# A two-layer hybrid attention block in float32: memory queries by way of DRAM, a scaling moved to ScalarE, two powers moved up, and the last tile cut 384 and 128

## The chip, the cores and the metric

The kernel runs on one core of a Trainium2 chip. The metric is the device time of one execution in microseconds (us). The profile is one execution taken by the hardware profiler. The engines are called PE (TensorE, with its weight loads as PEld), DVE (VectorE), ACT (ScalarE), POOL (GpSimd) and SP (SyncE, which here only issues transfers).

## What is computed

Two layers of a decoder trunk over 256 tokens of width 1024, everything in float32:

```python
h = rms_norm(x, norm_g[l])
q_a, k_a, v_a, q_h, f_h, i_h, q_m, z = jnp.split(h @ w_in[l], split_points, axis=-1)
# 8 heads x 64: QK-norm, partial rotary, causal softmax attention (one block of 256 keys)
qa = partial_rope(rms_norm(q_a, moba_q_norm[l]), positions)      # ka alike
o_a = moba_attention(qa, ka, va)
# 4 heads x 128: gated linear recurrence in chunks, then a norm of each head
o_h = rms_norm(hgrn2_chunkwise(q_h, f_h, i_h, lb_all[l]), hgrn_o_norm[l])
# 4 heads x 128: attention on 256 memory tokens
k_m, v_m = jnp.split(rms_norm(mem, mem_norm_g[l]) @ w_mem_kv[l], 2, axis=-1)
qm = rms_norm(q_m, mem_q_norm[l])                                # km alike
o_m = memory_attention(qm, km, v_m)                              # softmax(qm km^T / sqrt(128)) v_m
x = x + (jnp.concatenate([o_a, o_h, o_m], axis=-1) * jax.nn.silu(z)) @ w_out[l]
```

## The kernel before

**Weights.** All weights stream through the core once, in 60 chunks a layer of 128 x 1024 float32 (512 KB). Each takes the same road: SP loads it into `wr` (4 buffers; L177), ACT casts it to the rounded high part `wh` (3 buffers; L213, or L217 where a gain is folded in), DVE subtracts to get the low part `wl` (3 buffers; L227 or L231), and PE multiplies with both, so that high x high, low x high and high x low together give float32 accuracy. A chunk of `w_in` for a projection that is kept token by token (`group_b`, L292 to L294) takes 12 matmuls of 512 columns. The two gate projections at the end, ZA and ZM (`group_a`, L275), take 8 matmuls of 512 columns with `wh` and 8 of 256 with `wl` a chunk. The chunks of a layer, in order: 0 to 7 the memory's keys and values; 8 to 39 the projections F, Q, K, I, Q, Z of HGRN, the memory's queries (QM: 32 to 35) and VA (36 to 39); 40 to 43 ZA; 44 to 47 ZM; 48 to 59 `w_out` (L1443).

**What sets the order.** Each engine runs its instructions in the order in which they are written into its program. Generators for the side work (norms, rotary, recurrence, attention) are stepped between the matmul groups, and tables of the form `in_turn(a, b, c)` pin the order on DVE, ACT and POOL around named instructions: `("wl", c + 41)` is the low part of chunk 41 of layer `c / 60`, `("scale", 1, i)` a scaling of the second P, and so on.

**The memory's queries.** `g_qm` copies the QM projection to `qm` (L1246), takes sums of squares, and lets POOL raise the mean square to the power -1/2 (`rsq`, L702; `hgr` is the same for the recurrence's out-norm). `qm` holds a token per partition; the scores need a head's dimension per partition. So PE transposes it in 8 pieces of 128 x 128 (L1260, four for each half of the tokens) into a `sd` tile of PSUM, ACT casts the tile to `qmh` and DVE subtracts to `qml`. The 24 scores matmuls of a layer (L275, `sd<-kml,qmh` and the like) are written to run just after VA and within ZA.

**Trips through DRAM.** `across` (L85) turns other tensors: DVE transposes blocks of 32 x 32 within `src` into `blk` (L95), one transfer writes `blk` to a DRAM buffer `there` (L106), and four transfers of a quarter each bring it back in the turned layout (L111). All of a trip's transfers go by one queue, SP's or POOL's. The keys `kT` go by SP, and the queries `qT`, the recurrence's output `zh` and the softmax numerators P go by POOL. P comes in two halves of 128 x 1536 each (units 0 and 1); each is scaled by 1/sum (`ria`) on DVE in 8 pieces (L1178) ahead of its trip, and comes back as `PT`.

**Powers of K.** The key norm needs two powers on POOL (`rka`, L1081), one for each half of the tokens. In layer 0 POOL first finishes the rotary tables (L664 to L669), then raises both powers.

**The end.** In the last layer the last accumulator of `w_out` is cut into two parts of 256 columns, so that the first part's add (L1497) and output transfer start while PE works on the second (L1504).

Of the kernel before, what the change touches and what calls it, by code (L numbers as in the profile page):

```python
# [45 lines left out]
def hymba_kernel(ctx: ExitStack, tc: tile.TileContext, x, mem, mem_t, positions, w_in, w_out, w_mem_kv,  # L46
                 gains, moba_g, out):
    nc = tc.nc
# [39 lines left out]
    def across(dst, src, n, stage=None, free=None, name=None, q=None, behind=None, pace=(2, 4)):  # L88
# [21 lines left out]
        for c in (0, 2, 1, 3):  # L110
            ins = q.dma_start(dst[c * 32:c * 32 + 32], there[:, :, c].rearrange("q j r -> j q r"))  # L111
            if c == 2:
                yield
# [460 lines left out]
    def g_setup():  # L574
# [81 lines left out]
        for l in range(DEPTH):  # L656
            for q in (1, 0):
# [16 lines left out]
                if l == 0:  # L674
                    yield
# [201 lines left out]
    def g_hgrn(l):  # L877
# [60 lines left out]
        for m in (2, 8):  # L938
# [43 lines left out]
            nc.vector.tensor_tensor(Kn[:, :, 0:3], K4[:, :, 0:3], by(1, 3), op=OP.mult)  # L982
# [61 lines left out]
        for t in range(2):  # L1044
# [9 lines left out]
            yield  # L1054
        r = rsq("hg", ss, 8, 128)
# [12 lines left out]
    def g_qk(l, q, acc):  # L1068
# [8 lines left out]
        def spread(t):  # L1077
            t8 = slice(t * 8, t * 8 + 8)
            sumsq(ss[:, t8], acc[t], 8, "qk", t)
            nc.vector.tensor_scalar(ms[:, t8], ss[:, t8], 1.0 / 64, EPS, op0=OP.mult, op1=OP.add)  # L1080
            N["pow", t] = nc.gpsimd.tensor_tensor(r[:, t8], ms[:, t8], pw[:, :8], op=OP.pow)  # L1081
# [30 lines left out]
        else:  # L1112
            yield
            for t in range(2):
                k3 = heads(kr[:, t], 8)
                nc.vector.tensor_tensor(k3, k3, r[:, t * 8:t * 8 + 8][:, :, None].to_broadcast([128, 8, 64]),
                                        op=OP.mult)
# [41 lines left out]
    def g_moba_unit(l, u, P, mx):  # L1159
# [15 lines left out]
        for t in range(2):  # L1175
            for i in range(4):
                c = t * 4 + i
                N["scale", u, c] = nc.vector.tensor_scalar(P[:, i, kc[t]], P[:, i, kc[t]], ri[:, c:c + 1], None, op0=OP.mult)  # L1178
# [63 lines left out]
    def g_qm(l, acc):  # L1242
# [9 lines left out]
        yield 2  # L1252
        qmh = sb.tile([128, 4, 256], F32R, name="qmh", tag="ih", bufs=1)
        qml = sb.tile([128, 4, 256], F32R, name="qml", tag="hF", bufs=1)
        for t in range(2):
            ts = slice(t * 128, (t + 1) * 128)
            yield from room("sd")
            pt = side_tile()
            for h in range(4):
                N["qm turn", t, h] = nc.tensor.transpose(pt[:, h * 128:(h + 1) * 128], qm[:, t, h * 128:(h + 1) * 128],  # L1260
                                                         ident)
            N["qmh", t] = nc.scalar.copy(qmh[:, :, ts], heads(pt, 4))
            N["qml", t] = nc.vector.tensor_tensor(qml[:, :, ts], heads(pt, 4), qmh[:, :, ts].bitcast(F32), op=OP.subtract)
            rel()
        yield 2
# [95 lines left out]
    def order_of_attention(l):  # L1361
# [4 lines left out]
        in_turn(w("wl", 23), ("third", 8))  # L1366
# [3 lines left out]
        in_turn(w("wl", 26), ("decay", 8))  # L1370
# [11 lines left out]
        in_turn(w("wl", 37), w("wl", 38), ("across", f"turned0{l}"))  # L1382
        for h in range(4):
            in_turn(("mm", c + 37, 1, 1), ("qm turn", 1, h))
        if not l:
# [199 lines left out]
```

## Time and profile before

| | |
|---|---|
| median of 3 runs | 384.18 us (384.08 to 384.66) |
| the profiled execution | 384.07 us |
| its span in the profile | 382.3 us |
| PE busy | 377.0 us, 99% of the span |
| DVE, ACT, POOL busy | 322.7 us (84%), 251.0 us (66%), 113.5 us (30%) |
| moved by DMA | 87.64 MB, mean 229 GB/s |
| granted TensorE clock | 9 (of 9) in each of the 40 slices |

The profile's span runs from the first to the last recorded event; 1.8 us of the profiled execution's time lie outside it. Rows of the timeline, the chain of work that ended last and the groups of instructions give a start in us, a duration, the engine, the source line, and output<-inputs by the program's names. A group's row ends with the idle time in front of the group and who ended it.

### The profile page before, as it was taken

The page shows a single profiled execution, that of the slowest core. Times are in us where ns is not written, and L with a number is a line of the kernel's source. Part 1 is how long each engine was busy: PE and PEld are TensorE (multiplying, and loading weights), DVE is VectorE, ACT ScalarE, POOL GpSimd, SP SyncE. Part 2 cuts the span into 40 slices and gives each one's busy share as a digit, 9 for nine tenths or more (in the row PEclk, how much of TensorE's full clock was granted, in tenths as well). Part 3 has the DMA queues.
Part 4 walks back from the last instruction along what each step waited for, and adds up shares of the span by engine and source line. Part 5 has one row for each costly group of instructions (what it writes and reads, how often), then busy time and mean ns, then how long its engine had stood idle before and what let it go on. Part 6 is the DMA issues. An engine that isn't in the chain of part 4 may idle for free.

```text
span 382.3 us, 6807 instructions
## 1 busy us (share of the span) xinstructions
PE 377.0 (99%) x2431; PEld 317.6 (83%) x2431; DVE 322.7 (84%) x596; ACT 251.0 (66%) x428; POOL 113.5 (30%) x199
## 2 busy tenths in 40 slices
PE   8999999999999999999999999999999999999996
PEld 6888888878888888888888888888887888888885
DVE  4789979899879999967596989899897799998763
ACT  4988866449859839755366857455665993794540
POOL 3176889700700722320021030020043052225000
PEclk9999999999999999999999999999999999999999
DMA  8985795277923889996549668646766168999612
GB/s 268 418 319 180 229 308 167 111 256 227 294 106 120 269 275 330 333 256 227 172 171 286 213 210 245 238 135 227 261 220 223 55 247 262 321 303 318 204 53 110
DMA packets 27250, 87.64 MB, mean 229 GB/s; under 512 B 3792, under 2 KB 6224, under 8 KB 27216
## 3 DMA queue, kind: packets, MB, share of 16 engines
q1 hardware_dynamic: 22304, 71.31, 55.1%
q0 software_dynamic: 4624, 15.73, 13.9%
q8 instruction: 19, 0.31, 0.3%
q10 hardware_dynamic: 288, 0.15, 0.1%
q14 instruction: 15, 0.12, 0.1%
HBM read 76.18 MB, written 11.01 MB: 228 GB/s over the span
## 4 chain that ended last, share of the span: by engine, by line
PE 85%; POOL 9%; DVE 3%; issue 1%; DMA 1%; ACT 0%; DVEq 0%
PE acc L275 19%; PE acc L1443 17%; PE acc L312 12%; PE acc L292 9%; PE acc L293 9%; PE acc L294 9%; PE sd L275 5%; PE sd L279 4%; POOL rt L605 1%; POOL rt L606 1%; DMA gT<-in_gains_dram 1%; POOL mk L672 1%; POOL rtB L669 1%; POOL rk L721 1%; POOL rtA L666 1%
## 5 line engine op out<-in xcount | busy, mean ns | idle before, releaser
L213 ACT CAST wh<-wr 128x1024 fp32r<-128x1024 f32 x96 | 100.9, 1052 | 51.1 <-PE acc L275 15.6
L227 DVE TENSOR_TENSOR wl<-wr,wh 128x1024 fp32r<-128x1024 f32 x96 | 116.5, 1217 | 15.7 <-ACT wh L213 15.6
L293 PE MATMUL acc<-wl,hT 128*128 128x512 f32 x192 | 75.6, 394 | 0.0
L294 PE MATMUL acc<-wh,hT 128*128 128x512 f32 x192 | 74.8, 390 | 0.0
L292 PE MATMUL acc<-wh,hT 128*128 128x512 f32 x192 | 70.7, 396 | 0.0
L275 PE MATMUL acc<-hT,wh 128*128 128x512 f32 x256 | 63.9, 391 | 0.0
L275 PEld LDWEIGHTS acc<-hT,wh 128*128 128x128 f32 x256 | 46.4, 189 | 8.3
L292 PEld LDWEIGHTS acc<-wh,hT 128*128 128x128 f32 x192 | 35.9, 188 | 7.9 <-issue 0.7
L293 PEld LDWEIGHTS acc<-wl,hT 128*128 128x128 f32 x192 | 36.1, 188 | 7.7 <-DVE wl L227 0.7
L294 PEld LDWEIGHTS acc<-wh,hT 128*128 128x128 f32 x192 | 36.1, 188 | 7.5
L217 ACT ACTIVATE wh<-wr,gT 128x1024 fp32r<-128x1024 f32 (+1 forms) x29 | 28.7, 1006 | 12.9 <-DMA wr<-in_w_mem_kv_dram 6.2
L1443 PE MATMUL acc<-wl,yh 128*128 128x512 f32 (+1 forms) x96 | 37.1, 387 | 0.0
L1443 PE MATMUL acc<-wh,yl 128*128 128x512 f32 (+1 forms) x96 | 37.1, 387 | 0.0
L275 PEld LDWEIGHTS acc<-hT,wl 128*128 128x128 f32 x256 | 34.7, 190 | 2.2
L275 PE MATMUL acc<-hT,wl 128*128 128x256 f32 x256 | 35.4, 282 | 0.0
L231 DVE SCALAR_TENSOR_TENSOR wl<-wr,gT,wh 128x1024 fp32r<-128x1024 f32 (+1 forms) x29 | 31.1, 1094 | 5.0 <-ACT wh L217 5.0
L1443 PE MATMUL acc<-wh,yh 128*128 128x512 f32 (+1 forms) x96 | 30.6, 390 | 0.0
L106 POOL DMA_DIRECT2D there<-blk x9 | 5.8, 641 | 80.2 <-DVE hgm L700 39.1
L312 PE MATMUL acc<-wh,mTh 128*128 128x512 f32 x64 | 25.5, 402 | 0.3 <-ACT mTh L433 0.3
L312 PE MATMUL acc<-wh,mTl 128*128 128x512 f32 x64 | 25.1, 395 | 0.0
L1170 ACT ACTIVATE P<-P,nba,rq 128x128 f32<-128x128 f32 (+1 forms) x32 | 17.1, 546 | 9.1 <-DVE nba L1164 9.1
L1443 PEld LDWEIGHTS acc<-wh,yl 128*128 128x128 f32 x96 | 18.0, 188 | 3.7
(238 smaller groups left out, 650.6 us busy)
## 6 DMA issues: line engine op xcount, KB each, us to landing
wr<-in_w_in_dram SPq DMA_DIRECT2D x80, 512.0 KB, 4.2
wr<-in_w_out_dram SPq DMA_DIRECT2D x24, 512.0 KB, 6.7
wr<-in_w_mem_kv_dram SPq DMA_DIRECT2D x15, 512.0 KB, 5.3
there<-blk POOLq DMA_DIRECT2D x9, 512.0 KB, 4.7
there<-blk POOLq DMA_DIRECT2D x4, 768.0 KB, 6.4
PT<-there POOLq DMA_DIRECT2D x16, 192.0 KB, 5.4
there<-blk SPq DMA_DIRECT2D x4, 512.0 KB, 2.9
P<-there POOLq DMA_DIRECT2D x16, 128.0 KB, 6.4
```

The lines of the kernel that those rows point to most:

```text
L213: N["wh", i] = nc.scalar.copy(whs[i], raws[i])
L217: N["wh", i] = nc.scalar.activation(whs[i][:, sl], raws[i][:, sl], AF.Copy, scale=gT[:, g:g + 1])
L227: N["wl", i] = nc.vector.tensor_tensor(wls[i], raws[i], whs[i].bitcast(F32), op=OP.subtract)
L231: ins = nc.vector.scalar_tensor_tensor(wls[i][:, sl], in0=raws[i][:, sl], scalar=gT[:, g:g + 1], in1=whs[i][:, sl].bitcast(F32), op0=OP.mu ...
L275: nc.tensor.matmul(o, lhsT=a, rhs=b, start=s, stop=e)
L279: ins = nc.tensor.matmul(o, lhsT=a, rhs=b, start=s, stop=e)
L292: N["mm", i, j, t] = nc.tensor.matmul(acc[t], lhsT=th[:, k, ts], rhs=wH, start=k == 0, stop=False)
L293: N["mm l", i, j, t] = nc.tensor.matmul(acc[t], lhsT=th[:, k, ts], rhs=wL, start=False, stop=False)
L294: N["mm r", i, j, t] = nc.tensor.matmul(acc[t], lhsT=tl[:, k, ts], rhs=wH, start=False, stop=k == 7)
L312: N["kv", i, g, t, j] = nc.tensor.matmul(acc[g][t], lhsT=x[:, c, ts], rhs=y, start=c == 0 and j == 0, stop=c == 7 and j == 2)
L1170: N["exp", u, c] = nc.scalar.activation(P[:, i, kc[t]], P[:, i, kc[t]], AF.Exp, bias=nb[:, c:c + 1], scale=rq[:, r:r + 1], accum_out=sm[:, ...
L1443: ins = nc.tensor.matmul(a, lhsT=y, rhs=wt[:, cs], start=n == (0 if to is None else nk - 2) and j == 0, stop=n == nk - 1 and j == 2)
```

## The change

1. `qm` goes through DRAM with `across` (new parameter `back`: POOL writes it out, SP brings it back) in place of the 8 PE transposes a layer; ACT and DVE then read `qm` from SBUF. The trip's order on each engine is written into the tables.
2. ACT does the 8 scalings of the second P of each layer, in place of DVE.
3. In layer 0 POOL raises both powers of K before the rotary tables that are needed later.
4. The last accumulator is cut 384 and 128.
5. The tables for the stretch from VA to ZM are written anew: the maxima of the scores (`mxm`) move behind later weight chunks on DVE.

```diff
     def across(..., pace=(2, 4), back=None):
...
-            ins = q.dma_start(dst[c * 32:c * 32 + 32], there[:, :, c].rearrange("q j r -> j q r"))
+            ins = (back or q).dma_start(dst[c * 32:c * 32 + 32], there[:, :, c].rearrange("q j r -> j q r"))
...
+                if "pow10" in done:
+                    for j, o in enumerate(ops):
+                        N["later table", j] = o
+                        in_turn(("pow", 1, 1), ("later table", j))
...
+                if u:
+                    N["scale", u, c] = nc.scalar.mul(P[:, i, kc[t]], P[:, i, kc[t]], ri[:, c:c + 1])
+                else:
+                    N["scale", u, c] = nc.vector.tensor_scalar(P[:, i, kc[t]], P[:, i, kc[t]], ri[:, c:c + 1], None,
+                                                               op0=OP.mult)
...
-        yield 2
+        flat = qm.rearrange("p t s -> p (t s)")
+        while f"recurred{l}" not in done:
+            yield
+        yield from across(flat.rearrange("p (q r) -> p q r", q=4), flat, 8, "ih", q=nc.gpsimd, name=f"qm{l}", pace=(1, 1),
+                          back=nc.sync)
...
         for t in range(2):
-            ts = slice(t * 128, (t + 1) * 128)
-            yield from room("sd")
-            pt = side_tile()
-            for h in range(4):
-                N["qm turn", t, h] = nc.tensor.transpose(pt[:, h * 128:(h + 1) * 128], qm[:, t, h * 128:(h + 1) * 128],
-                                                         ident)
-            N["qmh", t] = nc.scalar.copy(qmh[:, :, ts], heads(pt, 4))
-            N["qml", t] = nc.vector.tensor_tensor(qml[:, :, ts], heads(pt, 4), qmh[:, :, ts].bitcast(F32), op=OP.subtract)
-            rel()
-        yield 2
+            N["qmh", t] = nc.scalar.copy(strip_of(qmh, t), strips(flat)[:, :, t])
+            N["qml", t] = nc.vector.tensor_tensor(strip_of(qml, t), strips(flat)[:, :, t],
+                                                  strip_of(qmh, t).bitcast(F32), op=OP.subtract)
+        yield
...
-                w("wl", 40), ("across", f"zh{l}"), ("qml", 1), *(("scale", 1, i) for i in range(8)), w("wl", 41),
-                ("across", f"turned1{l}"), ("mxm", 0, 0), w("wl", 42), ("mxm", 1, 0), w("wl", 43))
+                w("wl", 40), ("across", f"zh{l}"), ("qml", 0), w("wl", 41), ("qml", 1), w("wl", 42),
+                ("across", f"turned1{l}"), w("wl", 43))
...
-                both(t, c, 0, 256 if split else 512, True)
+                both(t, c, 0, 384 if split else 512, True)
...
-                    both(t, c, 256, 256, last, rest)
+                    both(t, c, 384, 128, last, rest)
```

What this does to the order, in layer 0 (layer 1 is alike, except for the powers). On DVE, from the low part of chunk 40, the place in the program stood so before (`wl_1647` is the low part of chunk 40, `wl_1685` of 41, `wl_1712` of 42, `wl_1765` of 43; `blk_1788` is the turned `zh`, `blk_1658` the turned second P):

```order
L227 TENSOR_TENSOR wl_1647<-wr_1490,wh_1591 128x1024
L95 STREAM_TRANSPOSE blk_1788<-zh_170 128x1024
L1263 TENSOR_TENSOR qml_1609<-sd_1617,qmh_1608 128x4x128
L1178 TENSOR_SCALAR P_1350<-P_1350,ria1_1514 128x128 x4
L1178 TENSOR_SCALAR P_1350<-P_1350,ria1_1514 128x256 x4
L227 TENSOR_TENSOR wl_1685<-wr_1540,wh_1645 128x1024
L95 STREAM_TRANSPOSE blk_1658<-P_1350 128x1536
L1293 TENSOR_REDUCE mxm0_1687<-sd_1661 128x2
L227 TENSOR_TENSOR wl_1712<-wr_1589,wh_1683 128x1024
L1293 TENSOR_REDUCE mxm1_1743<-sd_1717 128x2
L227 TENSOR_TENSOR wl_1765<-wr_1643,wh_1710 128x1024
```

The same place on DVE after the change (`wl_1645`, `wl_1683`, `wl_1710`, `wl_1763` and `wl_1804` are the low parts of chunks 40 to 44):

```order
L227 TENSOR_TENSOR wl_1645<-wr_1490,wh_1595 128x1024
L95 STREAM_TRANSPOSE blk_1786<-zh_170 128x1024
L1273 TENSOR_TENSOR qml_1630<-qm_1551,qmh_1629 128x4x128
L227 TENSOR_TENSOR wl_1683<-wr_1540,wh_1643 128x1024
L1273 TENSOR_TENSOR qml_1630<-qm_1551,qmh_1629 128x4x128
L227 TENSOR_TENSOR wl_1710<-wr_1593,wh_1681 128x1024
L95 STREAM_TRANSPOSE blk_1656<-P_1350 128x1536
L227 TENSOR_TENSOR wl_1763<-wr_1641,wh_1708 128x1024
L1303 TENSOR_REDUCE mxm0_1685<-sd_1659 128x2
L1303 TENSOR_REDUCE mxm0_1685<-sd_1660 128x2
L363 TENSOR_TENSOR as_1758<-acc_1732,al_1776 128x256
L227 TENSOR_TENSOR wl_1804<-wr_1679,wh_1761 128x1024
```

Both halves of `qml` now stand between `blk<-zh` and chunk 42, the scalings are gone from DVE, and the maxima stand behind chunk 43. Ahead of this place, a new `blk<-qm 128x1024` stands right after the low parts of chunks 37 and 38.

PE's order from the end of VA is now this (the high parts of chunks 40 and 41, the low part of 40, the high part of 42, the first scores, the high part of 43):

```order
L275 MATMUL acc<-hT,wh 128x512 x16
L275 MATMUL acc<-hT,wl 128x256 x8
L275 MATMUL acc<-hT,wh 128x512 x8
L275 MATMUL sd<-kml,qmh 128x256
L275 MATMUL sd<-kmh,qml 128x256
L275 MATMUL sd<-kmh,qmh 128x256
L275 MATMUL sd<-kml,qmh 128x256
L275 MATMUL sd<-kmh,qml 128x256
L275 MATMUL sd<-kmh,qmh 128x256
L275 MATMUL acc<-hT,wh 128x512 x8
```

Before, the first six scores stood right after the last matmul of VA (L294); they now follow 32 matmuls of ZA. The first six need the first half of the tokens only.

SP's queue in layer 0, from the keys' trip to the first chunks of `w_out` (the difference between the two; `wr` are the weight loads, the 12 run to chunk 42):

```order
 L111 DMA kT<-there 32x4x256 x4
-L177 DMA wr<-in_w_in_dram 128x1024 x17
+L177 DMA wr<-in_w_in_dram 128x1024 x12
+L111 DMA qm<-there 32x4x256 x4
+L177 DMA wr<-in_w_in_dram 128x1024 x5
 L177 DMA wr<-in_w_out_dram 128x1024 x12
```

The four return transfers of `qm` stand between the loads of chunks 42 and 43.

More of the change, by code (lines that the diff above doesn't have):

```diff
@@ L85, in small, with across @@
         return sb.tile([128, n], F32, name=name, tag=name, bufs=2)
-    def across(dst, src, n, stage=None, free=None, name=None, q=None, behind=None, pace=(2, 4)):
+    def across(dst, src, n, stage=None, free=None, name=None, q=None, behind=None, pace=(2, 4), back=None):
         q = q or nc.sync
@@ L673, in g_setup @@
                         in_turn(("table", 0, 1), ("mask of steps", j))
-                if l == 0:
-                    yield
+                    while "pow10" not in done:
+                        yield
     setup = g_setup()
@@ L1054, in g_hgrn @@
             yield
+        done.add(f"recurred{l}")
         r = rsq("hg", ss, 8, 128)
@@ L1080, in spread @@
             nc.vector.tensor_scalar(ms[:, t8], ss[:, t8], 1.0 / 64, EPS, op0=OP.mult, op1=OP.add)
-            N["pow", t] = nc.gpsimd.tensor_tensor(r[:, t8], ms[:, t8], pw[:, :8], op=OP.pow)
+            N["pow", t] = N["pow", q, t] = nc.gpsimd.tensor_tensor(r[:, t8], ms[:, t8], pw[:, :8], op=OP.pow)
+            if t:
+                done.add(f"pow{q}{l}")
         for t in range(2):
@@ L1365, in order_of_attention @@
         in_turn(w("wl", 22), ("decay", 2))
-        in_turn(w("wl", 23), ("third", 8))
+        in_turn(w("wl", 23), ("third", 8), ("scaled", 0), w("wl", 24))
         in_turn(w("wl", 24), ("fourth", 8))
@@ L1390, in order_of_attention @@
                 *(("scale", 0, i) for i in range(5)), ("ss", "h", 0), *(("scale", 0, i) for i in range(5, 8)),
-                ("ss", "h", 1), w("wl", 37), ("across", f"turned0{l}"), ("ms", "hg"), ("ss", "qm", 0),
-                ("ss", "qm", 1), w("wl", 39), ("qml", 0), ("ms", "qm"), *(("zh", i) for i in range(8)), ("ria", 1),
-                w("wl", 40), ("across", f"zh{l}"), ("qml", 1), *(("scale", 1, i) for i in range(8)), w("wl", 41),
-                ("across", f"turned1{l}"), ("mxm", 0, 0), w("wl", 42), ("mxm", 1, 0), w("wl", 43))
+                ("ss", "h", 1), w("wl", 37), w("wl", 38), ("across", f"qm{l}"), ("ms", "hg"), w("wl", 39), ("across", f"turned0{l}"),
+                ("ss", "qm", 0), ("ss", "qm", 1), ("ms", "qm"), ("ria", 1), *(("zh", i) for i in range(8)),
+                w("wl", 40), ("across", f"zh{l}"), ("qml", 0), w("wl", 41), ("qml", 1), w("wl", 42),
+                ("across", f"turned1{l}"), w("wl", 43))
         in_turn(*(("exp", 0, i) for i in range(5)), w("wh", 36), *(("exp", 0, i) for i in range(5, 8)),
                 ("sq", "h", 0), ("sq", "h", 1), w("wh", 37), ("qm", 0), ("sq", "qm", 0), w("wh", 38), ("qm", 1),
-                ("sq", "qm", 1), w("wh", 39), ("qmh", 0), *(("exp", 1, i) for i in range(8)), w("wh", 40), ("qmh", 1),
-                w("wh", 41), ("va", 0), w("wh", 42), ("va", 1), w("wh", 43))
+                ("sq", "qm", 1), w("wh", 39), *(("exp", 1, i) for i in range(8)), w("wh", 40),
+                w("wh", 41), ("va", 0), *(("scale", 1, i) for i in range(4, 8)), w("wh", 42), ("va", 1), ("qmh", 0),
+                w("wh", 43), ("qmh", 1), *(("scale", 1, i) for i in range(4)))
     def order_of_norm(l):
```

32 lines of the change are left out of this document (15 added, 17 removed).

## The prediction

> **What bounds the kernel now.** I read the page's first part, then the table of waits, then the chain of work that ended last and the timelines of DVE, ACT and POOL around the memory's queries.
>
> ```profile
> PE 377.0 (99%) x2431; PEld 317.6 (83%) x2431; DVE 322.7 (84%) x596; ACT 251.0 (66%) x428; POOL 113.5 (30%) x199
> ```
>
> PE is the bound: busy 377.0 us, 99% of the span. A step taken off PE pays in full, unless PE then waits for what it used to find ready. So the question is not what the transposes cost but whether DVE, the nearest to PE with 84%, and the transfers can follow a PE that is early.
>
> In the table of waits (waiter, what it waited for, us in total, times, longest), two rows belong to the powers of K, the wait of DVE for the powers and a wait of PE's weight loads for DVE's `hKb`:
>
> ```profile
> DVE kr L1116 <- POOL rka L1081: 1.6, 1, 1.6
> PEld sd L279 <- DVE hKb L891: 0.7, 1, 0.7
> ```
>
> That table has no wait of PE in the stretch from VA to ZM that is written anew.
>
> **The change, part by part. Transposes.** All 16 of them, by the tile they read, and the two groups of layer 0 in the chain of work that ended last:
>
> ```profile
> L1260 PE MATMUL sd<-ident,qm x16: 270/272/276, 120.7 to 309.1; 128*128 128x128 f32 x16
> ```
> ```profile
> 120.89 0.44 PE sd L1260 x4
> ...
> 123.61 0.44 PE sd L1260 x4
> ```
>
> Four groups of 0.44 us are on the path: -1.76 us, 0.88 a layer. Their casts to `qmh` and `qml` stay, now reading SBUF.
>
> **The trip in their place.** The rows that price it, first DVE's (layer 0), then ACT's:
>
> ```profile
> 119.66 2.35 DVE L227 TENSOR_TENSOR wl<-wr,wh 128x1024 fp32r<-128x1024 f32 x2
> ...
> 129.93 1.24 DVE L95 STREAM_TRANSPOSE blk<-zh 128x1024 f32<-128x1024 f32 x1
> 131.09 0.65 DVE L1263 TENSOR_TENSOR qml<-sd,qmh 128x512 fp32r<-128x512 f32 x1
> 131.66 1.91 DVE L1178 TENSOR_SCALAR P<-P,ria 128x128 f32<-128x128 f32 x8
> ...
> 142.82 1.22 DVE L227 TENSOR_TENSOR wl<-wr,wh 128x1024 fp32r<-128x1024 f32 x1
> ```
> ```profile
> 127.65 0.59 ACT L1262 CAST qmh<-sd 128x512 fp32r<-128x512 f32 x1
> ...
> 132.97 1.05 ACT L213 CAST wh<-wr 128x1024 fp32r<-128x1024 f32 x1 [1.85 <-PE acc L275]
> ```
>
> And the transfers, each from issue to landing: two of POOL's trips of 512 KB (at 92.8 and 278.2 us), then `zh`'s (132.0) and the first P's (124.0), then the returns of `kT` that SP issues (last row: of all eight, least, median, most).
>
> ```profile
> there<-blk POOLq DMA_DIRECT2D x1, 512.0 KB, 4.2
> ```
> ```profile
> there<-blk POOLq DMA_DIRECT2D x1, 512.0 KB, 3.6
> ```
> ```profile
> there<-blk POOLq DMA_DIRECT2D x1, 512.0 KB, 6.4
> ```
> ```profile
> there<-blk POOLq DMA_DIRECT2D x1, 768.0 KB, 4.9
> ```
> ```profile
> L111 SPq DMA_DIRECT2D kT<-there x8: 302/423/434, 83.2 to 269.1; - x8
> ...
> DMA to landing us min/median/max: 2.8/3.0/5.1
> ```
>
> `blk<-qm` starts when the low parts of 37 and 38 end, at 122.0, and takes the 1.24 of `zh`'s turn (same size): 123.2. POOL is free then; the issue stands ahead of the power `hgr`, which DVE needs only after P's turn. The way out is bounded by 3.6 and 6.4 us. I take 4.6, between the quiet 4.2 and the 4.9 of the larger transfer that leaves at this very place: 127.9. SP issues four returns at 0.42 each, the last at 129.2; bounded by 2.8 and 5.1, I take 3.5, since the median 3.0 comes from a stretch with less traffic: 132.7. The trip is then 9.4 us from issue at 123.3, with ends of 7.7 and 12.8. `qmh` for the first half takes 0.59: 133.3.
>
> **Does PE wait for the scores?** Rows of the chain:
>
> ```profile
> 129.54 0.48 PE sd L275 x4
> ```
> ```profile
> 130.27 1.59 PE acc L275 x7
> ...
> 135.22 19.51 PE acc L275 x112
> ```
>
> VA ends at 129.5 before, 0.9 earlier now: 128.6. A matmul of 512 columns takes 1.59/7 = 0.227; in the last row 56 of each kind make 19.51, so one of 256 takes 0.12. 24 x 0.227 + 8 x 0.12 = 6.4 us later, at 135.0, comes the first score. The first half's `qml` is ready at 133.3 + 0.65 = 134.0. No wait, with 1.0 us to spare. The cast of chunk 43 stands behind `qmh` on ACT: 134.3, needed after six scores at 135.7. Its load stands behind the four returns on SP, issued at 129.6 where it was 126.1, and with 4.3 us lands at about 133.9; the cast then ends at 134.9. Still in time, by 0.8.
>
> **DVE's new idle time.** `blk<-zh` ends at 129.93 + 1.24 = 131.2 before. Ahead of it the new turn comes in (+1.2) and the first `qml` drops out (-0.65): 131.7. `qml` can start at 133.3, so DVE idles 1.6 us there. What follows on DVE is rid of the scalings (-1.91) and pays the turn (+1.24) and the idle (+1.6): chunk 45's low part ends at 144.0 before (the last row of DVE's above) and 0.9 later now, while PE is 0.9 earlier. DVE falls back against PE by 1.8 us. Its next appointments with PE are at the start of `w_out`:
>
> ```profile
> 156.19 0.19 PEld L1443 LDWEIGHTS acc<-wl,yh 128*128 128x128 f32 x1
> ```
> ```profile
> 153.78 1.27 DVE L231 SCALAR_TENSOR_TENSOR wl<-wr,gT,wh 128x1024 fp32r<-128x1024 f32 x1
> ```
> ```profile
> 151.86 1.15 ACT L217 ACTIVATE wh<-wr,gT 128x1024 fp32r<-128x1024 f32 x1
> ```
>
> The low part of chunk 49 ends at 155.05 and PE takes it up with the weight load at 156.19, its matmul a quarter us after: 1.1 to 1.4 us to spare, say 1.3. Its high part ends at 153.01 and its first use is the third matmul of `w_out`, about 155.0: 2.0 to spare; its load is issued once chunk 45's low part has freed the buffer. 1.8 less 1.3 leaves a stall of about 0.5 us a layer: +1.0. It is nothing with an idle below 1.1 us, and grows one for one with a longer trip.
>
> **ScalarE's scalings** cost PE nothing by themselves: eight operations, each of half or a quarter of the columns of a `qmh` cast, so bounded by its 0.59 us. ACT's gap of 1.85 ahead of chunk 43's cast covers half of them. Four stand ahead of chunk 42's cast; with some 0.4 each, that cast ends near 131.6 and PE needs it 16 x 0.227 + 8 x 0.12 = 4.6 after 128.6, at 133.2. If that cover went, PE would wait for `wh` of 42.
>
> **The powers.** The wait of 1.6 on DVE for `rka` goes. What reaches PE is bounded by the difference of layer 0 and layer 1 over the same instructions, 54.31 - 53.34 = 0.97 us, and by nothing:
>
> ```profile
> 52.09:106.40 54.31, 54.01 (x482) 43.88 (x481) 48.71 (x82) 35.55 (x53) 29.25 (x50) 1.00 0.67 221
> 238.31:291.65 53.34, 53.34 (x481) 43.88 (x480) 48.73 (x83) 32.77 (x49) 10.93 (x11) 1.00 0.67 226
> ```
>
> I take 0.7, the wait for `hKb` above, which is the one that sits on DVE's late work: -0.7. Moved past the powers, the remaining tables end some 3 us later on POOL, whose next work is the trip at 92.8; that idle time hides them.
>
> **The last tile.** Before:
>
> ```profile
> 377.29 1.40 DVE L1497 TENSOR_TENSOR xs<-xs,acc 128x512 f32<-128x512 f32 x2 [0.67 <-PE acc L1443]
> 378.79 0.42 DVE L1504 TENSOR_TENSOR xs<-xs,sd 128x256 f32<-128x256 f32 x1
> ```
>
> The first part's six matmuls grow by half of 0.12 each, +0.35 on the add's start; the last add shrinks from 0.42 to about 0.28. The result is +0.2, less something for a transfer of 64 KB in place of 128: I take +0.1, with ends -0.1 and +0.3.
>
> **Sum:** -1.76 - 0.7 + 0.1 + 1.0 = -1.4 against the profiled 384.07: 382.7. The median of the runs shown is 0.11 above the profiled execution, so 382.8.
>
> **A rule against the trace.** The Trainium skill, "DMA: Bandwidth & Descriptors", section "Anatomy of one DMA", gives a POOL transfer about 2.0 us fixed and bytes over 436 GB/s. As an estimate from that page, 512 KB would take 3.2 us and a return 2.3, a trip of 6.8 us. The rows here, 3.6 to 6.4, are above it throughout; by the page the sum would be that of the second case below, -2.4.
>
> **The rivals.** *Short trip, no new wait (381.8).* With 3.6 + 1.3 + 2.8 = 7.7 us `qm` is back at 131.0; ACT then has the four scalings, chunk 42's cast and `va` ahead of `qmh`, which is done near 132.7, and DVE idles 1.0: below 1.1, no stall. -1.76 - 0.7 + 0.1 = -2.4. For it speak 4.2 and 3.6; against it the traffic:
>
> ```profile
> 130.00:135.00 5.00, 5.00 (x37) 4.69 (x36) 5.00 (x13) 2.44 (x4) 2.62 (x6) 1.00 0.83 203
> ```
>
> In these 5 us the DMA engines are busy for a share of 0.83 (the figure ahead of the GB/s), and the trip adds 1 MB a layer.
>
> *Long trip, slower (385.5).* PE waits for what DVE and ACT make from `qm`. Each us of trip beyond 9.4 costs each layer one us. The gain is gone at 9.4 + 0.7 = 10.1 us, and it is slower by more than 0.2% from 10.5. The 6.4 of `zh` alone, with 1.3 and 3.5, makes 11.2; a trip of 10.8 gives 382.7 + 2 x 1.4 = 385.5 and 12.8 would give 389.5. Against it: `zh` leaves 9 us later, into more traffic. The Trainium skill, "VectorE: DVE Perf Modes", section "Rules for kernel authors", speaks for this outcome: transpose 128 x 128 on TensorE if a PSUM destination will do. This trace has PE at 99%, which the rule does not weigh.
>
> *The second P comes back late (384.7).* POOL's timeline, the page's transfers and PE's weight loads:
>
> ```profile
> 150.46 2.23 POOL L111 DMA_DIRECT2D PT<-there  x4 [8.79 <-DMA there<-blk]
> ```
> ```profile
> PT<-there POOLq DMA_DIRECT2D x16, 192.0 KB, 5.4
> ```
> ```profile
> 160.13 1.49 PEld L279 LDWEIGHTS sd<-PT,va 128*64 128x64 f32 x19 [0.35 <-issue]
> ```
>
> The second P's way out waits 8.79 us to land; its last return is issued near 152.1 and lands near 157.5; PE loads it from 160.1, so some 2.6 us are to spare. PE's gain takes 0.9 of them and a POOL queue that reaches `zh`'s trip 0.8 later as much again. From a further 0.9 us on PE waits; an us of wait in each layer, +2.0, gives 384.7. That the shared engines were slow enough for it shows only in the 8.79.
>
> **How the numbers follow.** The likeliest case, a trip near 9.4 us, has 0.38, with a range of its own of 382.2 to 383.6. The short trip has 0.22, the long one 0.30, the late P 0.10. About 0.2% is what a measurement of this kernel can tell from no change: 383.4 and 384.95 are the limits. Faster: 0.33 of the first case and all of the second, 0.55. Same: 0.05, 0.10 of the long trip, 0.05 of the late P: 0.20. Slower: 0.20 and 0.05: 0.25. The range, 381.7 to 385.5, leaves out the upper part of the long trip (0.13) and a gain from the powers at its upper bound with a short trip (0.05).
>
> **What would show it.** PE's chain without L1260 and 0.88 less a layer between QM and VA; `qm<-there` landing near 132.7; DVE idle before the first `qml` by 1.6 us, ended by ACT's `qmh`; PE's first score without a wait near 135.0; a wait of about 0.5 us in the first eight matmuls of `w_out` for chunk 49; layer 0's window down to about 53.6; the last add at 379.0 in today's clock. The prediction is wrong if the trip is not within 8.7 to 10.1 us, or if PE waits for P near 160.

## The result and the profile after

| | before | after |
|---|---|---|
| median, four runs of each | 384.39 us (384.08 to 384.66) | 387.83 us (386.20 to 388.51) |
| the profiled execution, its span | 384.07, 382.3 us | 386.20, 384.4 us |
| moved by DMA | 87.64 MB | 89.73 MB |

The ratio is 1.0081 with a 95% interval of 1.0057 to 1.0105: slower, and above the range forecast. The profiled execution of the kernel after is the lowest of its four; its span is 2.1 us longer than before, and the traces can explain no more than this part of the 3.4 us. Executions more than 1.5% above the fastest of their kernel (four of those below, and one of the kernel before with 470.86 us) count in the medians and ranges given here, but not in the ratios.

PE has 16 instructions less and more idle time:

```profile
PE 378.1 (98%) x2415; PEld 315.2 (82%) x2415; DVE 321.7 (84%) x582; ACT 256.8 (67%) x444; POOL 116.2 (30%) x201
```

The chain of work that ended last, its shares by engine, has DVE with 12%; it had 3% before.

```profile
PE 81%; DVE 12%; ACT 3%; issue 1%; DMA 1%; SPq 0%; DVEq 0%
```

The table of waits (waiter, what it waited for, us in total, times, longest), first PE's weight loads, then DVE and ACT:

```profile
PEld acc L1451 <- DVE wl L231: 1.5, 3, 0.7
...
PEld acc L275 <- ACT wh L213: 1.0, 2, 0.6
PEld acc L293 <- DVE wl L227: 1.0, 2, 0.5
PEld acc L1451 <- ACT sg L846: 0.9, 2, 0.4
PEld acc L1451 <- DVE yl L133: 0.8, 2, 0.4
```
```profile
DVE qml L1273 <- ACT qmh L1272: 6.7, 4, 2.9
```

Four of the five rows of the weight loads are new. The row of L293 stood there before with 0.7 us in two; those were at 76.1 and 81.8, while now the two are in VA, 0.5 us each at 119.9 and 306.6. Each row comes about once a layer: the low part of a VA chunk (L293), the high part of ZA's chunk 43 (L275 from ACT), and, in the first half of `w_out` (L1451, the line that was L1443), the low parts of its first chunks and what is made from the gates. DVE's 6.7 us are the idle time ahead of the four `qml`.

DVE's timeline in layer 0, then in layer 1, and ACT's in layer 0 (start, duration, the idle time ahead in brackets):

```profile
133.70 0.69 DVE L1273 TENSOR_TENSOR qml<-qm,qmh 128x512 fp32r<-128x512 f32 x1 [2.90 <-ACT qmh L1272]
134.31 1.22 DVE L227 TENSOR_TENSOR wl<-wr,wh 128x1024 fp32r<-128x1024 f32 x1
135.96 0.69 DVE L1273 TENSOR_TENSOR qml<-qm,qmh 128x512 fp32r<-128x512 f32 x1 [0.43 <-ACT qmh L1272]
```
```profile
319.01 0.69 DVE L1273 TENSOR_TENSOR qml<-qm,qmh 128x512 fp32r<-128x512 f32 x1 [1.55 <-ACT qmh L1272]
...
322.64 0.69 DVE L1273 TENSOR_TENSOR qml<-qm,qmh 128x512 fp32r<-128x512 f32 x1 [1.80 <-ACT qmh L1272]
```
```profile
134.36 1.05 ACT L213 CAST wh<-wr 128x1024 fp32r<-128x1024 f32 x1 [0.69 <-PE acc L275]
135.31 0.61 ACT L1272 CAST qmh<-qm 128x512 fp32r<-128x512 f32 x1
```

The second `qmh` stands behind the cast of chunk 43, whose load stands behind the four returns on SP: it landed at 134.26 in layer 0 and 320.94 in layer 1, and the cast starts 0.1 us later in both. (Its row names PE, but PE's matmuls on the buffer that the cast takes over were done near 131.4 in layer 0, so it was the landing that ended the wait.) So chunk 43 is late for PE (0.3 and 0.6 us), and DVE waits for the second `qml` as well as for the first.

This idle time reaches PE. From the second `qml` on DVE has no break until it has made the low part of chunk 49, for which PE waits at the start of `w_out`. Busy time over the 20 us behind the second `qml`, in layer 0 and in layer 1 (PE, PEld, then DVE with 19.93), and the end of this stretch in the chain of work that ended last:

```profile
136.00:156.00 20.00, 19.92 (x121) 17.16 (x119) 19.93 (x34) 16.05 (x37) 5.56 (x10) 1.00 0.91 310
322.70:342.70 20.00, 19.90 (x121) 17.13 (x119) 19.93 (x34) 16.06 (x36) 5.55 (x10) 1.00 0.92 301
```
```profile
155.09 1.21 DVE wl L231
156.29 0.04 issue
156.34 1.20 PE acc L1451 x4
```

The way out of `qm`, issued at 122.45 (layer 0) and 309.22 (layer 1), KB and us to landing:

```profile
there<-blk POOLq DMA_DIRECT2D x1, 512.0 KB, 4.8
```
```profile
there<-blk POOLq DMA_DIRECT2D x1, 512.0 KB, 4.4
```

The last return landed at 132.95 and 318.26: trips of 10.5 and 9.0 us.

The traffic around it: busy time of each engine by 12 us of layer 0, the share of the DMA engines last but one; three rows of before, then the same of after.

```profile
130.00:142.00 12.00, 12.00 (x74) 10.72 (x73) 12.00 (x21) 4.92 (x7) 5.38 (x11) 1.00 0.88 255
142.00:154.00 12.00, 12.00 (x74) 10.66 (x73) 11.31 (x25) 11.15 (x26) 2.77 (x5) 1.00 0.92 313
154.00:166.00 12.00, 12.00 (x76) 9.82 (x75) 10.95 (x15) 7.33 (x12) 4.69 (x9) 1.00 0.98 322
```
```profile
130.00:142.00 12.00, 11.86 (x76) 10.46 (x76) 8.68 (x10) 6.42 (x13) 4.09 (x8) 1.00 0.95 311
142.00:154.00 12.00, 12.00 (x72) 10.42 (x71) 11.93 (x26) 10.81 (x27) 4.14 (x8) 1.00 0.91 318
154.00:166.00 12.00, 11.64 (x68) 8.46 (x67) 10.95 (x16) 8.16 (x12) 3.69 (x7) 1.00 0.94 322
```

From 130 to 166 us the DMA engines had little left before the change: .88 to .98. `zh`'s way out, a transfer that the change does not touch, takes 6.4 us before, and now:

```profile
there<-blk POOLq DMA_DIRECT2D x1, 512.0 KB, 8.1
```

PE's clock is 1.00 throughout. The table says when PE starts the same matmul in each profiled execution, less the time before (after 386.20 us, no trip 383.97, quarter trip 382.24, half trip 385.69, before plus the bytes 394.31). The kernels named in it follow below.

| | first K scores (84.2) | end of VA (128.9) | start of `w_out` (155.5) | middle of `w_out` (176.3) | layer 1: end of VA (314.2) | start of `w_out` (340.8) | middle (360.9) | near the end (377.6) |
|---|---|---|---|---|---|---|---|---|
| after | -0.99 | -1.60 | -0.82 | +0.39 | -0.24 | +0.56 | +2.03 | +2.27 |
| no trip | -0.88 | -1.50 | -1.52 | +0.31 | -0.32 | -0.35 | -0.21 | +0.02 |
| quarter trip | -1.09 | -1.42 | -1.44 | -1.29 | -1.87 | -1.90 | -1.79 | -1.55 |
| half trip | -0.85 | -1.47 | -1.48 | -0.34 | -0.96 | -0.67 | +1.80 | +2.04 |
| before plus the bytes | -0.02 | -0.04 | -0.03 | +6.73 | +6.73 | +6.72 | +10.34 | +10.33 |

After: 0.99 us are won at the powers and 0.61 in each layer by the transposes that are gone. Between the end of VA and the middle of `w_out` 1.99 us are lost in layer 0 and 2.27 in layer 1. The second P is not among the waits: its last return landed at 159.2 (157.5 before) and PE took it up at 160.5.

### The profile page after: what moved, and what is told of

It reads as the page before. It is cut to its first block, busy times and chain, and to the rows that moved or that the text cites. A ratio compares the mean times of both kernels' runs of the same rounds, so it can differ in the third digit from the quotient of the medians.

```text
span 384.4 us, 6802 instructions
## 1 busy us (share of the span) xinstructions
PE 378.1 (98%) x2415; PEld 315.2 (82%) x2415; DVE 321.7 (84%) x582; ACT 256.8 (67%) x444; POOL 116.2 (30%) x201
## 2 busy tenths in 40 slices
DMA packets 28690, 89.73 MB, mean 233 GB/s; under 512 B 3952, under 2 KB 7408, under 8 KB 28656
## 4 chain that ended last, share of the span: by engine, by line
PE 81%; DVE 12%; ACT 3%; issue 1%; DMA 1%; SPq 0%; DVEq 0%
PE acc L275 16%; PE acc L1451 16%; PE acc L312 11%; PE acc L293 10%; PE acc L294 10%; PE acc L292 10%; PE sd L279 4%; PE sd L275 3%; DVE wl L227 3%; ACT P L1178 2%; DVE P L1149 2%; DVE wl L231 1%; DVE mxm L1303 1%; DMA wr<-in_w_mem_kv_dram 1%; ACT wh L213 1%
## 5 line engine op out<-in xcount | busy, mean ns | idle before, releaser
L213 ACT CAST wh<-wr 128x1024 fp32r<-128x1024 f32 x96 | 100.4, 1052 | 37.5 <-PE acc L275 11.9
L293 PE MATMUL acc<-wl,hT 128*128 128x512 f32 x192 | 75.3, 392 | 0.1
L294 PE MATMUL acc<-wh,hT 128*128 128x512 f32 x192 | 74.8, 390 | 0.0
L275 PE MATMUL acc<-hT,wh 128*128 128x512 f32 x256 | 63.8, 392 | 0.6 <-ACT wh L213 0.4
L275 PEld LDWEIGHTS acc<-hT,wh 128*128 128x128 f32 x256 | 46.5, 189 | 9.5 <-ACT wh L213 1.0
L293 PEld LDWEIGHTS acc<-wl,hT 128*128 128x128 f32 x192 | 36.1, 188 | 8.1 <-DVE wl L227 1.0
L294 PEld LDWEIGHTS acc<-wh,hT 128*128 128x128 f32 x192 | 36.1, 188 | 7.5
L1451 PE MATMUL acc<-wl,yh 128*128 128x512 f32 (+1 forms) x96 | 37.5, 391 | 0.5 <-DVE wl L231 0.5
L1451 PE MATMUL acc<-wh,yl 128*128 128x512 f32 (+1 forms) x96 | 37.5, 391 | 0.2
L275 PEld LDWEIGHTS acc<-hT,wl 128*128 128x128 f32 x256 | 34.1, 190 | 2.4 <-DVE wl L227 0.6
L275 PE MATMUL acc<-hT,wl 128*128 128x256 f32 x256 | 35.3, 283 | 0.0
L1451 PE MATMUL acc<-wh,yh 128*128 128x512 f32 (+1 forms) x96 | 31.0, 394 | 0.1
L106 POOL DMA_DIRECT2D there<-blk x11 | 6.8, 622 | 75.6 <-DVE hgm L705 38.0
L1451 PEld LDWEIGHTS acc<-wl,yh 128*128 128x128 f32 x96 | 18.0, 188 | 5.0 <-DVE wl L231 1.5
```

Source lines behind the costliest of these rows:

```text
L213: N["wh", i] = nc.scalar.copy(whs[i], raws[i])
L275: nc.tensor.matmul(o, lhsT=a, rhs=b, start=s, stop=e)
L293: N["mm l", i, j, t] = nc.tensor.matmul(acc[t], lhsT=th[:, k, ts], rhs=wL, start=False, stop=False)
L294: N["mm r", i, j, t] = nc.tensor.matmul(acc[t], lhsT=tl[:, k, ts], rhs=wH, start=False, stop=k == 7)
L1451: ins = nc.tensor.matmul(a, lhsT=y, rhs=wt[:, cs], start=n == (0 if to is None else nk - 2) and j == 0, stop=n == nk - 1 and j == 2)
```

## The experiments

All were timed beside the kernel before on the same chip. "Ratio" is to that kernel, with a 95% interval.

**One part at a time.** Four kernels from the one before: the powers alone, the split alone, the trip with everything that belongs to it (scalings on ACT and the new tables too), and the scalings alone.

```diff
 powers only
+                if "pow10" in done:
...
+                        in_turn(("pow", 1, 1), ("later table", j))
 split only
-                both(t, c, 0, 256 if split else 512, True)
+                both(t, c, 0, 384 if split else 512, True)
...
 scalings only
+                if u:
+                    N["scale", u, c] = nc.scalar.mul(P[:, i, kc[t]], P[:, i, kc[t]], ri[:, c:c + 1])
...
```

> The kernel before with the powers of K early and nothing else. Theory 1 (the powers gain what layer 0 was behind layer 1, about 1.0 us, and the loss lies elsewhere): 383.2 to 383.5 and layer 0's window at 53.3 to 53.5 us. Theory 2 (the powers only move DVE's lateness to another place): 384.0 to 384.3.

> The kernel before with the last accumulator cut 384 and 128 and nothing else. Both theories: 384.3 to 384.6, 0.1 to 0.2 us above the kernel before, since the 128-wide end comes later by a longer first part and saves little behind it. If the smaller last transfer were worth more, 383.9 to 384.1.

> The change without the powers and without the 384 and 128: the trip, ScalarE's scalings and the tables. Theory 1 (all of the loss is here, and the powers' 1.0 us is simply added): 388.5 to 389. Theory 2 (the powers make PE early and so the trip late; without them the trip is less late against PE by 1 us in layer 0): 386.5 to 387.5.

> The kernel before with only the second P's scalings on ScalarE. If they cost nothing: the time of the kernel before within 0.3 us, or 0.1 to 0.3 us less. If ScalarE's casts of chunks 42 and 43 come late by them: 0.5 to 2 us more, with PE's waits on wh L213.

| | median (range, runs) | ratio |
|---|---|---|
| powers only | 383.25 (382.78 to 385.34, 12) | 0.9970 [0.9949, 0.9992] |
| split only | 384.21 (383.54 to 387.21, 12) | 1.0003 [0.9975, 1.0031] |
| trip only | 387.66 (385.95 to 391.45, 6) | 1.0103 [1.0062, 1.0144] |
| scalings only | 385.74 (383.33 to 387.49, 12) | 1.0015 [0.9987, 1.0043] |

The powers gain 1.1 us, the split and the scalings nothing that can be told. The median of the scalings is 0.9 us higher, but of the 1.9 us that their profiled execution is late, 1.5 are lost in the first 9 us of the span, long before a scaling, and no row shows PE waiting for ACT's cast (L213). The whole loss is in the trip with what belongs to it. Of the kernels that compute the right values, the powers alone are the fastest.

**Is it the place of load 43?** The returns are issued behind load 43 in place of ahead of it:

```diff
+        while back is not None and st["dma"] < 60 * int(name[-1]) + 44: yield
```

> The changed kernel with chunk 43's load ahead of the four returns on SP. Theory 1 (DVE idles ahead of the second qml because chunk 43's cast on ACT waits for that load): PE's wait for chunk 43's high part (0.4 and 0.6 us) goes, the second idle of DVE (0.4 and 1.8 us) falls below 0.3, and the time to 385 to 386.3, 1.5 to 2.5 us less than the changed kernel's median. Theory 2 (the length of the trip alone sets the loss): 387.5 to 388.

387.46 us (385.42 to 389.45, 7 runs), ratio 1.0081 [1.0050, 1.0112]: nothing gained. The idle time ahead of the second `qml` is gone, but now `qm` is late: the way out took 6.1 us (7.4 in layer 1), and the first `qml` waits longer.

```profile
134.57 0.69 DVE L1274 TENSOR_TENSOR qml<-qm,qmh 128x512 fp32r<-128x512 f32 x1 [3.41 <-ACT qmh L1273]
```

In layer 1 PE itself waits for it:

```profile
PE sd L276 <- ACT qmh L1273: 1.9, 1, 1.9
```

Whichever of the two stands first, the other is late.

**Is it the wait for the way out, or DVE's wait for `qml`?** Two kernels on the one after. In the first the returns read from the input `x` and so need not wait for the way out (the queries in the memory are other numbers). In the second both `qml` stand behind chunks 41 and 42 on DVE, and the second `qmh` ahead of chunk 43 on ACT.

```diff
 no wait for the way out
-            ins = (back or q).dma_start(dst[c * 32:c * 32 + 32], there[:, :, c].rearrange("q j r -> j q r"))
+            ins = (back or q).dma_start(dst[c * 32:c * 32 + 32], there[:, :, c].rearrange("q j r -> j q r") if back is None else dram(x, c * 256, [[1024, 32], [32768, 4], [1, 256]]))
 late qml
-                w("wl", 40), ("across", f"zh{l}"), ("qml", 0), w("wl", 41), ("qml", 1), w("wl", 42),
+                w("wl", 40), ("across", f"zh{l}"), w("wl", 41), w("wl", 42), ("qml", 0), ("qml", 1),
-                w("wh", 43), ("qmh", 1), *(("scale", 1, i) for i in range(4)))
+                ("qmh", 1), w("wh", 43), *(("scale", 1, i) for i in range(4)))
```

> The changed kernel, but the four returns read the same number of bytes from the input x, so they do not wait for the way out to land; all transfers still run, and the memory's queries are not the right ones. Theory 1 (the loss is DVE's idle time ahead of the two qml, 3.3 us a layer, which the trip causes): qm is back near 126 us, both idles fall below 1 us, no wait at the start of w_out, 381.7 to 382.7. Theory 2 (the extra megabyte on the DMA engines, the new order or ScalarE's scalings cost it, whatever the trip's length): 385 to 388.

> The changed kernel with both qml on DVE behind the low parts of chunks 41 and 42, and both qmh on ACT ahead of chunk 43's high part; the trip and its transfers stay as they are. Theory 1 (what the trip costs is the idle time of the engines behind it, not its length): DVE's idle ahead of qml falls from 3.3 to about 0.7 us a layer, the waits at the start of w_out go, 382 to 383.5. Theory 2 (the trip's length or the extra traffic costs by itself): 386 to 388.

Both are slower still: 391.22 us (390.32 to 392.46, 6 runs), 1.0165 [1.0128, 1.0202], and 391.92 us (390.97 to 394.85, 6 runs), 1.0190 [1.0149, 1.0232]. Each took only a part of DVE's idle time away. In the first, 0.65 us are left at the first `qml` of each layer, and 1.64 and 1.32 at the second. In the second, 0.4 us are left at the `qml` in all, but DVE now idles at its next step, the turn of P, for the scalings on ACT (2.09 us in layer 0, 1.69 in layer 1):

```profile
137.00 1.78 DVE L95 STREAM_TRANSPOSE blk<-P 128x1536 f32<-128x1536 f32 x1 [2.09 <-ACT P L1187]
```

PE's wait has moved to the second P and to the chunks of `w_out`. PE in the first, then in the second:

```profile
PE sd L279 <- DMA PT<-there: 3.4, 2, 2.5
PE acc L1451 <- ACT wh L217: 1.8, 1, 1.8
```
```profile
PE sd L279 <- DMA PT<-there: 4.1, 2, 2.3
```

In the second kernel the loads of chunks 45 and 46 leave at 132.2 and 133.3, where in the kernel after they leave at 135.6 and 137.9. `zh`'s way out runs beside them and takes 10.6 us (8.1); the second P's way out, behind it on POOL's queue, leaves at 145.7 (142.9), and the second P lands at 164.2 (159.2). In the first kernel the returns run beside the first P's way out, which takes 7.7 us (3.7); `zh`'s and the second P's (9.6) come late behind it, and the second P lands at 164.0. So taking the idle time away lets transfers run into each other; in the kernel after it also kept them apart. That the idle time costs nothing where it stands does not follow.

**Wait or bytes?** Two kernels on the one after. One does the same work in the same order but leaves out the five transfers (the turned queries are not carried). The other keeps them, but the returns land in a tile that nobody reads there, so ACT and DVE need not wait for them (the queries are read unturned).

```diff
 no trip
+            q.dma_start(there.rearrange("q j c r -> (q j) c r"), blk) if back is None else None
+        for c in (0, 2, 1, 3) if back is None else ():
...
 traffic nobody waits for
-        yield from across(flat.rearrange("p (q r) -> p q r", q=4), flat, 8, "ih", q=nc.gpsimd, name=f"qm{l}", pace=(1, 1),
+        yield from across(zT[M_].rearrange("p (q r) -> p q r", q=4), flat, 8, "ih", q=nc.gpsimd, name=f"qm{l}", pace=(1, 1),
```

> The changed kernel without the five transfers of the trip: the turn on DVE stays, and qmh and qml read qm as it stands, so the scores are those of unturned queries; the order on every engine is otherwise the same. If the trip (its bytes or its length) is the whole loss: 381.5 to 382.5, the gain of the transposes (1.76 less two waits of 0.33 for the low part of a VA chunk) and of the powers (1.0). If the new order of the tables or ScalarE's scalings are part of it: 384 or more.

> The changed kernel with the whole trip, but the four returns land in a buffer that nobody reads before 150 us, and qmh and qml read qm as it stands: the bytes and SP's wait without the engines' wait. Theory A (the loss is the idle time that the wait for qm makes on DVE): 381.7 to 383. Theory B (the loss is a megabyte more a layer on DMA engines that are nearly full, which makes P, the weights or qm late, whichever is issued last): 386 to 391, with PE waiting for PT near 160 or for chunk 49.

No trip: 383.85 us (382.12 to 389.63, 12 runs), 0.9980 [0.9946, 1.0014]. Traffic that nobody waits for: 389.19 us (385.63 to 392.96, 10 runs), 1.0085 [1.0053, 1.0118], as slow as the kernel after. Without the transfers the loss is gone, so it comes from them. That the new order and the scalings on ACT cost nothing is not shown as clearly: of the 2 us that powers and transposes were expected to gain, the median keeps 0.8, and the interval is 1.3 us wide to each side. In the profiled execution of no trip PE loses 1.8 us once, in the first layer, with a wait for what DVE makes of the memory's P:

```profile
PEld sd L279 <- DVE mP L198: 1.9, 1, 1.9
```

Without it that execution would be where the quarter trip is. The second is not clean: load 43 still stands behind the returns, landed at 135.8, and DVE waited for the second `qmh` behind it (2.62 us in layer 0, 2.78 in layer 1), so that its idle time at the four `qml` is 6.7 us, as in the kernel after. So the bytes were tried by themselves, below.

**The bytes alone, on the kernel before.** Order and transposes are those of before. SP also issues, between the loads of chunks 42 and 43, what a trip moves:

```diff
+            if i in (42, 102):
+                spare = away.tile([4, 32, 4, 256], F32, name="spare", tag="spare", bufs=2)
+                load(spare.rearrange("q j c r -> (q j) c r"), xs[:, 0].rearrange("p (c r) -> p c r", c=4))
+                for c in range(4):
+                    load(zT[M_][c * 32:c * 32 + 32].rearrange("j (q r) -> j q r", q=4), dram(x, c * 256, [[1024, 32], [32768, 4], [1, 256]]))
```

> The kernel before, in its own order and with its 16 transposes, plus per layer the bytes of the trip as traffic that nobody waits for: SP issues, beside load 42, one write of 512 KB to a DRAM buffer and four reads of 128 KB into a tile that is not read there. Nothing of the computation is changed. Bytes theory: the DMA engines are .88 to .98 busy from 130 to 166 us in the profile before, so the 1 MB makes a chunk of w_out, a query copy or the second P late; 386 to 389 us, with new waits of TensorE of 0.4 us or more between 135 and 166 us. Waiting theory (the loss is VectorE's wait for qml): no instruction waits for these bytes, 384.0 to 384.7 us.

391.38 us (389.01 to 394.31, 6 runs) against 383.97, ratio 1.0171 [1.0137, 1.0205]. Load 43 was issued at 126.4, as before the change (126.1), so SP's queue is not the reason. No step of the computation waits for these bytes, and yet PE waits for the second P in both layers (its L284 is L279 above):

```profile
PE sd L284 <- DMA PT<-there: 6.2, 2, 3.9
```

The trips on POOL's queue follow one another, and each takes longer: the first P's way out 8.0 us (4.9 before), `zh`'s 8.1 (6.4), the second P's 8.9 (8.7). The second P lands at 165.7, where it landed at 157.5.

The profiled execution is the slowest of the six, so its rows show the place, and the ratio the size. At the least, 389.01, it is 5 us slower. Part of the spread is PE's clock (last section): the mean granted clock is 0.991 in the profiled one, 0.996 in two, and 0.999 to 1.000 in the three that took 389.0 to 391.0 us. A megabyte a layer at this place thus costs more than the kernel after loses. That kernel wins some of it back with the powers and the transposes, and its returns are spread over more time (they wait for the way out, where here all five transfers are issued from 122.4 to 125.3); how much each of the two makes was not parted.

**The dose.** The kernel after with a quarter of the trip (128 KB out, one return) and with half (256 KB, two returns), both waited for; the rest of the queries is not carried.

```diff
 quarter (half: 2 in place of 1, and (0, 1) in place of (0,))
+            q.dma_start(there.rearrange("q j c r -> (q j) c r")[:, :4 if back is None else 1], blk[:, :4 if back is None else 1])
+        for c in (0, 2, 1, 3) if back is None else (0,):
```

> The changed kernel with a quarter of the trip: 128 KB out and one return of 128 KB, for which qmh waits; the rest of qm is read as it stands. Theory A: the wait stays for the length of two short transfers, some 5 to 6 us, so qm is back near 128 to 129 and 382 to 384. Theory B (bytes): 382 to 383. Here the two differ in what PE waits for: by A DVE ahead of qml, by B nothing.

> The kernel after with half of the trip: 256 KB go out and two of the four returns of 128 KB come back, both waited for as before; the other half of the queries in the memory is not carried (their values are those left in the tile). Bytes theory: between the quarter trip (0.9972 of the kernel before) and the whole trip (1.0081), at about 1.001 to 1.004, so 384.8 to 386.2 us. Waiting theory: the way out and the last return come as late as with the whole trip less one or two issues of 0.4 us, so at least 386.5 us.

| moved more, a layer | median (range, runs) | ratio |
|---|---|---|
| nothing | 383.85 (382.12 to 389.63, 12) | 0.9980 [0.9946, 1.0014] |
| 256 KB | 384.46 (381.53 to 388.04, 12) | 0.9972 [0.9941, 1.0003] |
| 512 KB | 384.45 (382.44 to 388.18, 12) | 1.0013 [0.9985, 1.0042] |
| 1 MB | 387.83 (386.20 to 388.51, 4) | 1.0081 [1.0057, 1.0105] |

Each row was timed beside runs of its own of the kernel before, so the ratios compare and not the medians. Up to 512 KB no loss can be told; with 1 MB there is one. The quarter trip's way out took 5.3 us in layer 0, no less than the whole one's 4.8 (in layer 1 3.7 and 4.4):

```profile
there<-blk POOLq DMA_DIRECT2D x1, 128.0 KB, 5.3
```

But its one return is back at 130.8, two us before the last of the whole trip's four, and load 43 behind it is earlier too. From the end of VA to the middle of `w_out` the quarter trip loses 0.13 and 0.08 us (the table above), the half trip 1.13 and 2.76. The dose does not part wait from bytes, since both shrink together. The kernel before with the bytes added shows what bytes alone can cost, but not which of the two the kernel after pays.

**What the idle time costs.** The prediction has a rule for this: up to 1.1 us of idle time a layer costs PE nothing, and each us beyond that costs one. DVE's idle time ahead of the two `qml` and PE's loss from the end of VA to the middle of `w_out`, in us, layer 0 / layer 1:

| profiled execution | idle time | less 1.1 | PE's loss |
|---|---|---|---|
| after | 3.33 / 3.35 | 2.23 / 2.25 | 1.99 / 2.27 |
| trip only | 2.66 / 2.92 | 1.56 / 1.82 | 1.36 / 1.62 |
| load 43 first, layer 0 | 3.41 | 2.31 | 2.01 |
| half trip, layer 0 | 2.43 | 1.33 | 1.13 |
| quarter trip | 0.87 / 0.63 | 0 / 0 | 0.13 / 0.08 |

The rule holds to within 0.3 us in these. Elsewhere other things hold PE up. With load 43 first, layer 1 has 5.46 us of idle time and loses 4.41, nearly all before `w_out`, where PE waits for the first scores. PE loses more than the rule says in the half trip's layer 1 (idle time 2.20, loss 2.76; PE waits there also for the second P and the memory's P), in layer 0 of no trip (the memory's P), in the two kernels with a late second P, and, by up to 0.7 us, in the traffic that nobody waits for.

## Why the prediction was wrong

- *Transposes, -1.76.* The matmuls went, but only 0.61 of the 0.88 a layer stayed at the end of VA: PE came early to the low part of a VA chunk, the wait of L293 above (1.0 in two, 0.3 of it each in the matmuls' starts). The prediction looked for DVE's next appointment with PE at the start of `w_out`; this one stands before the trip begins to count.
- *Powers, -0.7.* -0.99 in the profiled execution and -1.1 in the run of its own: the upper bound, the difference between the layers, was the right row.
- *Last tile, +0.1.* Nothing that can be told: 1.0003.
- *Scalings on ACT cost PE nothing.* Nothing that can be told: 1.0015 by themselves, and no wait of PE for ACT's casts.
- *The trip, 9.4 us.* 10.5 and 9.0; layer 0 lies outside the 8.7 to 10.1 that the prediction had set for itself. The way out was 4.8 and 4.4 for 4.6: well sized. The returns took longer in layer 0. DVE idled 2.9 and 0.4 us there, and 1.55 and 1.80 in layer 1, where 1.6 was said, at the first `qml` alone; the scores themselves cost PE 0.3 at most, in layer 0. By the prediction's own rate the mean of 9.75 would cost 0.7 us more than its sum, which is -0.7 and not +2.1: the length alone does not explain the loss. The Trainium skill, "DMA: Bandwidth & Descriptors", section "Anatomy of one DMA", gives 2.0 us and bytes over 436 GB/s, an estimate of 3.2 us for 512 KB and 2.3 for 128 KB; measured on POOL's queue were 4.4 to 4.8 and 3.7 to 5.3, and the short trip did not come.
- *Chunk 43 in time by 0.8.* It was late by 0.3 and 0.6. Load 43 was issued at 129.4 and landed at 134.3, close to what was said (133.9); the cast started at 134.36 and ended at 135.4, and PE was 1.60 us early at the end of VA, where 0.9 was reckoned. That the second `qmh` stands behind this cast, and the second `qml` and the low parts behind it, was missed.
- *A stall of 0.5 a layer at `w_out`.* 1.21 and 1.47 between its start and its middle, for the low parts as said, and for the gates and `yl` too.
- **The step that failed:** the size of DVE's idle time. The prediction put it at 1.6 us a layer, at the first `qml` alone; 3.33 and 3.35 were measured. In layer 0 the longer trip made 2.90 of it at the first `qml`. At the second, which the prediction did not price, DVE waited 0.43 and 1.80 more, behind load 43, which stands behind the returns. By the prediction's own rule this is a stall of 2.2 us a layer and not 0.5, and 1.99 and 2.27 were measured. Together with -0.99 for the powers and -0.61 a layer for the transposes it makes the +2.1 of the profiled execution. So the mechanism was the right one, and this term was sized at half.
- **A cost that was left out:** what the trip's transfers cost the others. The share of 0.83 was quoted against the short trip alone, and only the case called "the second P comes back late" had this mechanism, with a chance of 0.10 and one us a layer. In the profiled execution of the kernel after it is not among PE's waits. It shows as soon as the order gives way: with less idle time at the `qml`, or with the bytes alone, the second P lands at 164 to 166 us and PE waits for it. The bytes alone make 5 us or more in both layers together. So none of the orders that were tried makes the trip pay.

What stays open: no run has the wait without the traffic, so in the kernel after the two are told apart by its chain and by the idle times, not by an experiment. Its median is 1.6 us above the execution that was profiled, and what its longer runs wait for was not seen. All kernels spread (the one before from 383.2 to 387.9 in 24 runs, the quarter trip from 381.5 to 388.0); in two longer executions that were profiled, the scalings alone and the traffic that nobody waits for, some 1.5 us were lost in the first 9 us of the span. Whether it is the bytes that count or the packets (the four returns come in 512 of 1 KB) was not parted. The profiled quarter trip, with -1.55 us near the end, shows that what was forecast for PE can be reached without most of the trip; its ratio, 0.9972, has an interval that reaches 1.

## What to carry to other kernels

Before a matmul or a transpose is traded for a transfer, list all that comes to stand behind its return: on each engine that reads it, and in the queue that issues it. Here the second `qml`, behind the load behind the four returns, made 2.2 of DVE's 6.7 us of idle time and had no price. Then read the share of the DMA engines over the next 40 us, not only over the transfer: with .9 and more, 1 MB made the second P late though nobody waited for the new transfers. Adding the bytes alone to the kernel before shows what they can cost. And where PE is made early, list every low part it takes up from that point on, beginning with the very next.

## What the runs showed of the hardware

PE's clock fell by half after idle times of a few us. In the kernel before with the bytes added, PE was idle from 161.9 to 165.8; busy time by 1 us, the clock third from the end of the row:

```profile
163.00:164.00 1.00, 0.00 (x0) 0.00 (x0) 1.00 (x2) 0.00 (x0) 0.00 (x0) 1.00 1.02 418
164.00:165.00 1.00, 0.00 (x0) 0.00 (x0) 0.32 (x2) 0.89 (x2) 0.00 (x0) 0.54 1.02 417
...
169.00:170.00 1.00, 1.00 (x3) 0.79 (x3) 0.43 (x1) 0.54 (x1) 0.69 (x2) 0.50 0.88 344
170.00:171.00 1.00, 1.00 (x4) 0.73 (x3) 0.69 (x1) 0.08 (x1) 0.78 (x2) 0.55 0.98 295
171.00:172.00 1.00, 1.00 (x6) 0.84 (x5) 0.00 (x0) 0.00 (x0) 0.88 (x2) 1.00 0.78 209
```

The mean of 0.54 from 164 to 165 puts the fall at about 164.1, some 2.2 us after PE fell idle. Some 5 us of work at half speed, an estimated loss of 2.5 us, followed the wait of 3.9 us; together they are most of the 6.7 us that PE was late there. With the returns behind load 43, the clock fell to 0.50 from 324 to 327 us, after idle times of 1.9 and 0.3 us. The Trainium skill, "TensorE: Matmul & The Clock Gate", section "What's actually happening", has the half rate after an idle window of about 3.4 us that runs freely; the 0.50 agrees, but here the fall came after 2.2 us, and once after 1.9 and 0.3, while waits of 2.3 us (layer 1 of this kernel, and layer 0 of the one with both `qml` late) left the clock at 1.00.
